# First part's arrays laid out by the host, the second pointwise product's bias as full products, and layer 0's VectorE adaLN tiles as row sums

## The chip, the core and the metric

The kernel runs on one core of a Trainium2 chip. The core has five engines with queues of their own: TensorE (PE, matrix products; its weight loads are listed as PEld), VectorE (DVE), ScalarE (ACT), GpSimd (POOL) and SyncE (SP), which here issues almost all DMAs. They share an on-chip memory (SBUF) of 128 partitions; products go to a second one (PSUM) in banks of 128 x 512 fp32. The metric is the device time of one execution in microseconds; lower is better. The profile is one execution, recorded by the hardware.

## The reference, cut to what matters

A trunk of two layers on 256 tokens of width 2048, all in fp32. Layer 0 mixes tokens by a convolution module, layer 1 by differential attention; both are followed by an MLP of hidden width 8192. Every sub-layer is shifted, scaled and gated by vectors computed from one condition vector c (adaLN):

```python
cond = jax.nn.silu(c)
for i in range(DEPTH):
    mod = cond @ ada_w[i] + ada_b[i]                 # 2048 x 12288 per layer
    sh_m, sc_m, g_m, sh_f, sc_f, g_f = [m[:, None, :] for m in jnp.split(mod, 6, axis=-1)]
    h = x * (1.0 + sc_m) + sh_m
    y = conformer_conv(h, ...) if i % 2 == 0 else diff_attention(h, ...)
    x = layer_norm(alpha * x + g_m * y, ln_mix_g[i], ln_mix_b[i])
    h = x * (1.0 + sc_f) + sh_f
    y = squared_relu_mlp(h, ...)
    x = layer_norm(alpha * x + g_f * y, ln_ffn_g[i], ln_ffn_b[i])

def conformer_conv(h, w1, b1, w_dw, b_dw, g, b, w2, b2):
    u = h @ w1 + b1                                  # first pointwise product, 2048 -> 4096
    a, gt = jnp.split(u, 2, axis=-1)
    u = a * sigmoid(gt)
    u = depthwise_causal_conv(u, w_dw, width=31) + b_dw
    u = silu(layer_norm(u, g, b))
    return u @ w2 + b2                               # second pointwise product, 2048 -> 2048
```

Most of the work is products with weights that are read once: per layer the adaLN matrix (100 MB), the mixer's weights and the MLP's.

## The kernel before

**Products.** fp32 operands are split into a high part in a faster fp32 format and the rest: ACT casts 128 x 1024 of raw weights to the high part (L552 in the first product, L613 behind it), DVE subtracts to get the low part (L553, L615), and PE adds three products per 128 x 512 tile: high x high, high x low, low x high (L564 to L566, L653 to L656). `mm_parts` and `run_jobs` do this for two tiles of 128 tokens.

**The first part** is written out by hand: the order of PE, DVE, ACT and SP is as in the program text (`manual_schedule`). Because h needs shift and scale of the adaLN first, the 2048 input channels are taken in six slices of 128, 128, 256, 512, 512 and 512 (`SLICES`, s = 0 to 5). For each slice the kernel computes the adaLN shift and scale for its channels, makes h from x, and adds the slice's share of the first pointwise product to sums in SBUF (`add_up`, L1106) for eight groups of 2 x 256 output columns. While PE multiplies slice s, the adaLN tiles of slice s + 1 are worked off at set steps (`PAIR_AT`); at the end of a slice come the mod vectors (`end_ada`) and the next slice's h (`put_h`).

**adaLN tiles** come as raw tiles of 1 MiB, through a list of items (`items`, `load_ahead`, `ada_next`) loaded in order on SP's queue into a few rotating homes. Three ways to work them off stand in the kernel:
- by PE (`ada_slice_steps`, `ada_both_steps`): products of the condition (repeated to 32 columns, `condr`) with the tile, then a transpose and a reduction;
- by DVE in layer 0 (`ada_slice_dve_steps`, L253, L255): multiply each chunk of 128 input rows by its condition value and add into an accumulator of nf x 128 columns; at the end PE sums over partitions with products against ones (L238) and DVE adds the bias. This is used for the scale of slices 4 and 5, and later for g_m (channels 0 to 7), sc_f (all 16) and sh_f (0 to 3): 36 channels of 128 columns;
- by DVE in layer 1 and part of g_f (`ada_steps`, L382): the host has laid the matrix out by output column (`ada_rows`), so one instruction multiplies a 128 x 2048 tile by the condition, broadcast to all partitions, and accumulates each row to one value.

**x** is loaded by tokens, in four pieces (`X_AT`), into z; PE transposes each 128 x 128 piece (`put_h1` L1074, `to_featT` L492); DVE and ACT apply scale and shift from PSUM (L501, L504, L1079), ACT and DVE split the result (`put_split`). Then ACT multiplies z by alpha (`alpha_x`, L1064) for the residual. The small vectors and the taps of the convolution come as rows, in 17 small loads (`load_small`), and are turned to columns by PE (`as_cols` L134, `tap_columns` L949).

**Behind the slices** come the convolution on PE (L880), its LayerNorm and swish, and the second pointwise product (`out_proj` with `pw2`), where DVE and PE work off the rest of layer 0's adaLN tiles. Its bias is added by two products with four rows each (L652: four rows of bias as high and low part, picked by a column of the identity), before each of 4 x 2 accumulations. `add_gated` (L823, L824) multiplies by the gate and adds to z.

From there on the order of PE and DVE is still that of the program text; that of ACT, POOL and SP is chosen by a planner that simulates the program when it is built.

## Time and profile before

| | us |
|---|---|
| median of 3 runs | 2330.64 |
| lowest, highest | 2330.64, 8066.31 |
| the profiled execution, whole | 2329.99 |
| its span (first to last instruction) | 2327.4 |
| PE busy in the span | 2267.9 (97%) |
| DVE busy | 1744.0 (75%) |
| ACT busy | 1085.6 (47%) |
| POOL busy | 148.7 (6%) |
| moved by DMA | 607.53 MB, 261 GB/s over the span |
| mean granted clock of PE | 0.995 |

How to read the profile: a group of instructions is named by its line, engine, operation and tiles (output <- inputs), with partitions x elements; behind it stand the count, the busy time, the mean in ns of one, and the idle time before them with what ended it. Matmuls are pipelined, and the duration of one holds its latency: in a row of them each holds PE for less than its duration. A row of the waits says which engine waited at which line for what: sum in us, times, longest. A row of the chain of waits or of the timeline begins with the start and the length in us. A row of a window gives its ends, its length, then busy time (and count) of PE, PEld, DVE, ACT and POOL, then the granted clock (1.00 is full), the DMA share and GB/s.

### The profile page before, as it was taken

The numbers are of one execution on the slowest core, as the hardware profiler recorded it, in microseconds if no ns is written. First come the engines' busy times: TensorE is split into PE (matmuls) and PEld (weight loads), VectorE is DVE, ScalarE is ACT, GpSimd is POOL, SyncE is SP. The second block draws the span as 40 slices with busy tenths as digits, with TensorE's granted clock in tenths as the row PEclk, the third lists the DMA queues.
The fourth block names the chain that finished last, engine by engine and source line by source line (L and its number), as shares of the span: only waits on it lengthen the run. The fifth ranks groups of instructions, "written<-read, shape, count | busy, mean of one in ns | idle before, by whom it ended". The sixth has DMA issues, their size and how long they took to land.

```text
span 2327.4 us, 28629 instructions
## 1 busy us (share of the span) xinstructions
PE 2267.9 (97%) x11183; PEld 1807.8 (78%) x11183; DVE 1744.0 (75%) x2116; ACT 1085.6 (47%) x1497; POOL 148.7 (6%) x110
## 2 busy tenths in 40 slices
PE   7999989999999999999999999999999999999999
PEld 4676647778788888888878888877788888888886
DVE  5687788878887888877878877887975655655556
ACT  3344674365345345445454445545444443443442
POOL 0000001102200000000004110110310000000000
PEclk9999999999999999999999999999999999999999
DMA  9997489969998988888847665784966556565563
GB/s 343 375 347 284 169 305 377 329 241 340 340 326 302 321 288 317 316 298 308 311 159 260 243 210 180 275 310 156 317 234 211 181 185 199 181 199 189 191 218 108
DMA packets 264319, 607.53 MB, mean 261 GB/s; under 512 B 11105, under 2 KB 24567, under 8 KB 249463
## 3 DMA queue, kind: packets, MB, share of 16 engines
q1 hardware_dynamic: 264040, 605.67, 74.4%
q8 instruction: 87, 1.43, 0.2%
q14 instruction: 48, 0.39, 0.0%
q10 hardware_dynamic: 144, 0.06, 0.0%
HBM read 603.53 MB, written 2.15 MB: 260 GB/s over the span
## 4 chain that ended last, share of the span: by engine, by line
PE 74%; issue 16%; DVE 6%; ACT 2%; DMA 2%; POOL 0%; POOLq 0%; DVEq 0%; ACTq 0%; SPq 0%
PE w_ps L656 18%; PE w_ps L655 18%; PE w_ps L653 18%; DVE wl_w L615 2%; PE pw_ps L653 1%; PE qkv_q_ps L656 1%; PE qkv_q_ps L653 1%; PE qkv_q_ps L655 1%; PE qkv_v_ps L656 1%; PE qkv_v_ps L653 1%; PE qkv_v_ps L655 1%; PE ut L1425 1%; PE pw_ps L656 1%; DVE adaw L382 1%; PE pw_ps L655 1%
## 5 line engine op out<-in xcount | busy, mean ns | idle before, releaser
L615 DVE TENSOR_TENSOR wl_w<-w_w,wh_w 128x1024 fp32r<-128x1024 f32 x510 | 634.4, 1262 | 337.1 <-ACT wh_w L613 336.8
L613 ACT CAST wh_w<-w_w 128x1024 fp32r<-128x1024 f32 x512 | 536.1, 1053 | 693.7 <-PE w_ps L656 524.2
L653 PE MATMUL w_ps<-wh_w,hm_hi 128*128 128x512 f32 x1024 | 402.1, 393 | 2.4 <-ACT hm_hi L474 2.4
L656 PE MATMUL w_ps<-wh_w,hm_lo 128*128 128x512 f32 x1024 | 399.6, 390 | 1.6 <-DVE hm_lo L477 1.6
L655 PE MATMUL w_ps<-wl_w,hm_hi 128*128 128x512 f32 x1024 | 399.5, 390 | 1.5 <-DVE wl_w L615 1.5
L655 PE MATMUL w_ps<-wl_w,u_hi 128*128 128x512 f32 x1024 | 399.0, 390 | 1.2 <-DVE wl_w L615 1.1
L653 PE MATMUL w_ps<-wh_w,u_hi 128*128 128x512 f32 x1024 | 399.5, 390 | 0.0
L656 PE MATMUL w_ps<-wh_w,u_lo 128*128 128x512 f32 x1024 | 398.6, 389 | 0.0
L382 DVE SCALAR_TENSOR_TENSOR adaw<-adaw,cond_rows 128x2048 f32<-128x2048 f32 x108 | 249.9, 2314 | 0.5 <-DMA adaw<-in_ada_rows_dram 0.5
L653 PEld LDWEIGHTS w_ps<-wh_w,hm_hi 128*128 128x128 f32 x1024 | 192.6, 188 | 43.9 <-ACT hm_hi L474 3.9
L656 PEld LDWEIGHTS w_ps<-wh_w,hm_lo 128*128 128x128 f32 x1024 | 192.6, 188 | 42.9 <-DVE hm_lo L477 2.9
L655 PEld LDWEIGHTS w_ps<-wl_w,u_hi 128*128 128x128 f32 x1024 | 192.3, 188 | 42.6 <-DVE wl_w L615 3.1
L655 PEld LDWEIGHTS w_ps<-wl_w,hm_hi 128*128 128x128 f32 x1024 | 192.8, 188 | 41.5 <-DVE wl_w L615 2.4
L653 PEld LDWEIGHTS w_ps<-wh_w,u_hi 128*128 128x128 f32 x1024 | 192.3, 188 | 39.8
L656 PEld LDWEIGHTS w_ps<-wh_w,u_lo 128*128 128x128 f32 x1024 | 192.2, 188 | 39.9
L564 PE MATMUL pw_ps<-wh_pw,h_hi 128*128 128x512 f32 x256 | 107.3, 419 | 9.8 <-ACT wh_pw L552 3.5
L565 PE MATMUL pw_ps<-wl_pw,h_hi 128*128 128x512 f32 x256 | 103.0, 403 | 5.1 <-DVE wl_pw L553 5.1
L566 PE MATMUL pw_ps<-wh_pw,h_lo 128*128 128x512 f32 x256 | 102.2, 399 | 0.0
L553 DVE TENSOR_TENSOR wl_pw<-w_pw,wh_pw 128x1024 fp32r<-128x1024 f32 x64 | 77.5, 1220 | 19.8 <-ACT wh_pw L552 19.7
L552 ACT CAST wh_pw<-w_pw 128x1024 fp32r<-128x1024 f32 x64 | 65.7, 1050 | 41.3 <-PE pw_ps L566 27.4
L564 PEld LDWEIGHTS pw_ps<-wh_pw,h_hi 128*128 128x128 f32 x256 | 49.4, 193 | 40.2 <-issue 16.3
L565 PEld LDWEIGHTS pw_ps<-wl_pw,h_hi 128*128 128x128 f32 x256 | 49.5, 193 | 16.2 <-DVE wl_pw L553 7.2
(372 smaller groups left out, 3125.8 us busy)
## 6 DMA issues: line engine op xcount, KB each, us to landing
w_w<-in_mlp_w_dram SPq DMA_DIRECT2D x256, 1024.0 KB, 5.5
adaw<-in_ada_rows_dram SPq DMA_DIRECT2D x108, 1024.0 KB, 6.7
aw<-in_ada_w_dram SPq DMA_DIRECT2D x40, 1024.0 KB, 9.1
w_pw<-in_conv_pw_w_dram SPq DMA_DIRECT2D x64, 512.0 KB, 10.5
conv_ux<-in_ada_w_dram SPq DMA_DIRECT2D x17, 1024.0 KB, 8.3
w_pw<-in_conv_pw_w_dram SPq DMA_DIRECT2D x16, 1024.0 KB, 5.2
w_qkv_q<-in_attn_qkv_w_dram SPq DMA_DIRECT2D x16, 1024.0 KB, 5.9
w_qkv_k<-in_attn_qkv_w_dram SPq DMA_DIRECT2D x16, 1024.0 KB, 5.1
```

The costliest lines, as they stand in the source:

```text
L382: nc.vector.scalar_tensor_tensor(w, w, 1.0, late["cond"], ALU.mult, ALU.mult, accum_out=st["m"][:, ch:ch + 1])
L552: nc.scalar.copy(hq, rq)
L553: nc.vector.tensor_tensor(lq, rq, hq.bitcast(F32), op=ALU.subtract)
L564: nc.tensor.matmul(pss[t], lhsT=xh, rhs=wh, start=(kc == first), stop=False)
L565: nc.tensor.matmul(pss[t], lhsT=xh, rhs=wl, start=False, stop=False)
L566: nc.tensor.matmul(pss[t], lhsT=xl, rhs=wh, start=False, stop=(kc == last))
L613: nc.scalar.copy(hi, rq)
L615: eng.tensor_tensor(lo, rq, hi.bitcast(F32), op=ALU.subtract)
L653: nc.tensor.matmul(pss[tt], lhsT=xh, rhs=wh, start=(kc == 0 and job["bias"] is None), stop=False)
L655: nc.tensor.matmul(pss[tt], lhsT=xh, rhs=wl, start=False, stop=False)
L656: nc.tensor.matmul(pss[tt], lhsT=xl, rhs=wh, start=False, stop=(kc == nk - 1))
L1425: nc.tensor.transpose(out=pt[:, j * P:(j + 1) * P], in_=us[:, j * P:(j + 1) * P], identity=ident)
```

## The change

- **Layout by the host** (`lay_out`): x also by channels (`x_t`), the small vectors as columns in two arrays (`cols_first`, `cols_rest`), the taps as columns, layer 0's PE adaLN tiles and the first product's weight tiles each as one array of 128 x 2048 in the order of use (8 KB in one piece per partition, where pieces had 512 bytes to 4 KB), and 36 more channels in `ada_rows`.
- **h from x by channels** (`chunk_h`): scale and shift read xT in SBUF; no transposes. xT lies in z's buffer; x by tokens is loaded into z once, at step 9 of the last slice, and not scaled: `add_gated` of the second product multiplies by alpha in its add.
- **Row sums** (`dot`, `ada_slice_dot_steps`): layer 0's 36 DVE channels are worked off as layer 1's, one instruction per tile; the bias is added by DVE right behind the last (`add_bias`). The condition as rows (`cond_rows`) is now made at the start, by 16 products with the identity, instead of being written to memory and read back behind the second product.
- **The bias of the second product**: high part in partitions 0 to 3 and low part in 32 to 35 of a zeroed 128 x 512 tile, and one product with 128 rows (`one` has a 1 in row q and in row 32 + q) instead of two with 4.
- A scratch buffer (`R`) moves to the pool that is opened later.

```diff
-X_AT = {(0, 0): (256, 512), (2, 1): (512, 1024), (3, 4): (1024, 2048)}
+X_AT = {(0, 0): (2, 4), (2, 1): (4, 8), (3, 4): (8, 16)}
...
+def lay_out(inputs):
...
+    return {
+        "cols_first": cols(i["c"], i["ada_b"][0]),
+        "cols_rest": cols(i["ada_b"][1], i["conv_pw1_b"], i["conv_dw_b"], i["conv_ln_g"], i["conv_ln_b"],
+                          i["mlp_b1"], i["ln_mix_g"][0], i["ln_mix_b"][0], i["ln_ffn_g"][0], i["ln_ffn_b"][0],
+                          i["ln_mix_g"][1], i["ln_mix_b"][1], i["mlp_b2"], i["attn_subln_g"]),
+        "x_t": i["x"][0].T.reshape(KC, P, S).transpose(1, 0, 2),
+        "taps_t": taps, "ada_tiles": np.stack(ada),
+        "ada_rows": np.stack([at[l][v, ch] for l, v, ch in row_specs()]), "pw1_tiles": np.stack(pw1),
+    }
...
+    vec0 = const.tile([P, KC + 6 * KC], F32, name="vec0")
+    nc.sync.dma_start(vec0, cols_first)
...
+    cond_rows = const.tile([P, D], F32, name="cond_rows")
+    for q in range(4):
+        pt = mm_bank(f"cond_p{q}")
+        for j in range(4):
+            nc.tensor.matmul(pt[:, j * P:(j + 1) * P], lhsT=cond[:, 4 * q + j:4 * q + j + 1].broadcast_to([P, P]),
+                             rhs=ident, start=True, stop=True)
+        if q % 2:
+            nc.scalar.copy(cond_rows[:, q * NG:(q + 1) * NG], pt)
+        else:
+            nc.vector.tensor_copy(cond_rows[:, q * NG:(q + 1) * NG], pt)
+
+    def dot(w, m, ch):
+
+        nc.vector.scalar_tensor_tensor(w, w, 1.0, cond_rows, ALU.mult, ALU.mult, accum_out=m[:, ch:ch + 1])
+
+    def add_bias(m, i, v, c0, n):
+        nc.vector.tensor_tensor(m[:, c0:c0 + n], m[:, c0:c0 + n], adab[i][:, v * KC + c0:v * KC + c0 + n], op=ALU.add)
...
+    xT = z.rearrange("p t (a n) -> p (t a) n", n=S)
...
-            pt = tp_tile(f"apt_{i}_{v}_{f0}")
-            for f in range(nf):
-                nc.tensor.matmul(pt[:, f:f + 1], lhsT=st["acc"][:, f * P:(f + 1) * P], rhs=ones[:, 0:1],
-                                 start=True, stop=True)
...
-                nc.vector.scalar_tensor_tensor(st["acc"], wv[:, kc % per, :], cond[:, kc:kc + 1],
-                                               st["acc"], ALU.mult, ALU.add)
...
+        def load(ch):
+            st[ch] = ada_raw(f"ad_{v}_{ch}")
+            nc.sync.dma_start(st[ch], ada_rows[ADA_ROWS[0, v, ch]])
...
+        def step(ch):
+            dot(st.pop(ch), m, ch)
+            if ch == f0 + nf - 1 and not first:
+                finish()
...
+    def chunk_h(mul, add, c0, n):
+
+        h32 = [work.tile([P, 1, S], F32, tag="B", name=f"h0_h{c0 + j}") for j in range(n)]
+        for j in range(n):
+            cc = c0 + j
+            if j == 0:
+                nc.vector.tensor_scalar(h32[j][:, 0, :], xT[:, cc, :], mul[:, cc:cc + 1], add[:, cc:cc + 1],
+                                        ALU.mult, ALU.add)
+            else:
+                nc.scalar.activation(h32[j][:, 0, :], xT[:, cc, :], AF.Identity,
+                                     scale=mul[:, cc:cc + 1], bias=add[:, cc:cc + 1])
+        for j in range(n):
+            put_split(hT, c0 + j, 1, 0, S, h32[j])
...
-        rv = raw.rearrange("p (a h n) -> p a h n", a=src.shape[1], h=2)
-        for h in range(2):
-            raws["dma"] = nc.sync.dma_start(rv[:, :, h, :], src[:, :, h, :])
+        raws["dma"] = nc.sync.dma_start(raw, pw1_tiles[n])
...
-        nc.vector.tensor_tensor(z[:, t, sl], z[:, t, sl], tmp, op=ALU.add)
+        if times is None:
+            nc.vector.tensor_tensor(z[:, t, sl], z[:, t, sl], tmp, op=ALU.add)
+        else:
+            nc.vector.scalar_tensor_tensor(z[:, t, sl], z[:, t, sl], times, tmp, ALU.mult, ALU.add)
...
-            nc.scalar.activation(z[:, t, sl], z[:, t, sl], AF.Copy, scale=ALPHA)
...
+        hl = work.tile([P, NG], F32R, tag="X", name="pw2b_hl", bufs=3)
+        nc.gpsimd.memset(hl.bitcast(F32), 0.0)
+        for p0 in (0, 32):
+            with tc.issue_after(raws["dma"].ins):
+                nc.sync.dma_start(rows[p0:p0 + 4, :], conv_pw2_b[0].rearrange("(q n) -> q n", n=NG))
+            nc.scalar.copy(hl[p0:p0 + 4, :], rows[p0:p0 + 4, :])
+        nc.vector.tensor_tensor(hl[32:36, :], rows[32:36, :], hl[32:36, :].bitcast(F32), op=ALU.subtract)
+        one = small.tile([P, 4], F32R, tag="one4", name="one4", bufs=1)
+        nc.vector.tensor_tensor(one, ident[:, 0:4], ident[:, 32:36], op=ALU.add)
...
+                nc.sync.dma_start(vec1, cols_rest)
+                nc.sync.dma_start(wct.rearrange("p a k b -> p (a k b)"), taps_t)
+            elif (s, h) == (5, 9):
+                nc.sync.dma_start(z, x[0].rearrange("(t p) d -> p t d", p=P))
...
-             bias=lambda q: lambda: [(bias0["one"][:, q:q + 1].broadcast_to([4, P]), bias0["hl"][:, n, :])
-                                     for n in range(2)])
+             bias=lambda q: lambda: [(bias0["one"][:, q:q + 1].broadcast_to([P, P]), bias0["hl"])])
...
-        late["cond"] = late["pool"].tile([P, D], F32, tag="acc", name="cond_rows")
-        with tc.issue_after(raws["dma"].ins):
-            nc.sync.dma_start(late["cond"], cond_mem.rearrange("k p -> (k p)").partition_broadcast(P))
...
-            aT = work.tile([P, S], F32, tag="R", name=f"{nm}_aT", bufs=3)
+            aT = late["pool"].tile([P, S], F32, tag="R", name=f"{nm}_aT", bufs=3)
```

More of the change, by code (lines that the diff above doesn't have):

```diff
@@ L60 @@
 ON_ACT = (0, 2, 3, 5, 6, 8, 9, 11, 13, 14)
-DVE_WAIT = 3
 ALPHA = (2.0 * DEPTH) ** 0.25
@@ L73, with ada_specs @@
 PI_IN = 3.1415925
-ADA_ROWS = {key: n for n, key in enumerate([(0, G_F, ch) for ch in range(4, KC)] + [
-    (1, v, ch) for v in range(6) for ch in range(KC)])}
+def ada_specs():
+    out = []
+    for s, (f0, nf) in enumerate(SLICES):
+        if s < BOTH_PE and 2 * nf * P <= NG:
+            out += [("both", f0, nf, a) for a in range(2 * nf)]
+        else:
+            out += [(v, f0, nf, a) for v in ((SC_M, SH_M) if s < BOTH_PE else (SH_M,)) for a in range(nf)]
+    for v, f0, nf in ((G_M, 8, 4), (G_M, 12, 4), (SH_F, 4, 4), (SH_F, 8, 4), (SH_F, 12, 4), (G_F, 0, 4)):
+        out += [(v, f0, nf, a) for a in range(nf)]
+    return out
@@ L271, in ada_slice_steps @@
+            add_bias(m, 0, v, f0, nf)
+        def step(ch):
+            dot(st.pop(ch), m, ch)
+            if ch == f0 + nf - 1 and not first:
+                finish()
+        loads = [lambda ch=ch: load(ch) for ch in range(f0, f0 + nf)]
+        steps = [lambda ch=ch: step(ch) for ch in range(f0, f0 + nf)]
+        return (loads, [[f] for f in steps], finish) if first else (loads, steps)
     def ada_slice_steps(i, v, f0, nf, m, first=False, apart=False):
@@ L1058, in ada_pair @@
         later.append(rest)
-    def alpha_x(q):
-        sl = slice(q * NG, (q + 1) * NG)
-        for t in range(NT):
-            nc.scalar.activation(z[:, t, sl], z[:, t, sl], AF.Copy, scale=ALPHA)
     def end_ada(s):
@@ L1068, in end_ada, with put_h @@
             f()
-    def put_h1(s):
-        c0 = SLICES[s][0]
-        pt = tp_tile(f"h0_t1_{c0}")
-        for t in range(NT):
-            nc.tensor.transpose(out=pt[:, t * P:(t + 1) * P], in_=z[:, t, c0 * P:(c0 + 1) * P], identity=ident)
-        def rest():
-            nc.vector.tensor_scalar(mul[:, c0:c0 + 1], m_sc[:, c0:c0 + 1], 1.0, None, ALU.add)
-            h32 = work.tile([P, 1, S], F32, tag="B", name=f"h0_h1_{c0}")
-            nc.vector.tensor_scalar(h32[:, 0, :], pt[:, :S], mul[:, c0:c0 + 1], m_sh[:, c0:c0 + 1],
-                                    ALU.mult, ALU.add)
-            put_split(hT, c0, 1, 0, S, h32)
-        return rest
-    def put_h(s, c2, now=True):
-        f0, nf = SLICES[s]
-        made = put_h1(s) if nf == 1 else to_featT(z, hT, mul, m_sh, "h0", [c2])
-        def rest():
-            if nf > 1 and 2 * c2 == f0:
-                nc.vector.tensor_scalar(mul[:, f0:f0 + nf], m_sc[:, f0:f0 + nf], 1.0, None, ALU.add)
-            made()
-            if nf > 1 and c2 % 2:
-                later.append(lambda: alpha_x(c2 // 2))
-        if now:
-            rest()
-        return rest
+    def put_h(s, c2):
+        f0, nf = SLICES[s]
+        c0, n = (f0, 1) if nf == 1 else (2 * c2, 2)
+        if c0 == f0:
+            nc.vector.tensor_scalar(mul[:, f0:f0 + nf], m_sc[:, f0:f0 + nf], 1.0, None, ALU.add)
+        chunk_h(mul, m_sh, c0, n)
     def add_up(g, s, pss):
@@ L1129, in pw2_bias @@
     def pw2_bias():
[L1131 to L1138 removed]
+        rows = work.tile([P, NG], F32, tag="bc_b2", name="pw2b", bufs=1)
+        hl = work.tile([P, NG], F32R, tag="X", name="pw2b_hl", bufs=3)
[7 more added lines that the diff above has]
+        nc.vector.tensor_tensor(one, ident[:, 0:4], ident[:, 32:36], op=ALU.add)
         bias0.update(hl=hl, one=one)
@@ L1206, in trunk @@
                 split_half(s)
-            if s == 3 and 5 <= h < 9:
-                tap_columns(h - 5)
-            elif (s, h) == (3, 9):
-                conv_vectors()
+            if (s, h) == (3, 5):
+                nc.vector.tensor_reduce(eye, ident.rearrange("p (r c) -> p c r", c=32), axis=AX.X, op=ALU.add)
             if h in PAIR_AT[s]:
@@ L1319, in ln_t, with out_proj @@
         return [stats, norm]
-    def out_proj(pair, w2d, gate, name, pump, at_end, start=None, hold=False, on_pool=((),) * 4, bias=None):
+    def out_proj(pair, w2d, gate, name, pump, at_end, start=None, hold=False, on_pool=((),) * 4, bias=None,
+                 times=None):
         st = stats_tile(name)
@@ L1722, in fin_begin @@
         fin["zg"] = big.tile([P, NT, D], F32, tag="hTl", name="fin_zg")
-        fin["rows"] = late["pool"].tile([P, D], F32, tag="acc", name="fin_rows")[0:2]
+        fin["rows"] = cond_rows[0:2]
         fin["cols"] = small.tile([P, NT, 2], F32, tag="fcol", name="fin_cols", bufs=1)
```

236 lines of the change are left out of this document (62 added, 174 removed).

## The prediction

> **What bounds the kernel now.** I read the page first (spans, the chain), then the busy time by stage, then the waits of TensorE inside the first stages, and last single stretches of the timeline.
>
> ```profile
> span 2327.4 us, 28629 instructions
> PE 2267.9 (97%) x11183; PEld 1807.8 (78%) x11183; DVE 1744.0 (75%) x2116; ACT 1085.6 (47%) x1497; POOL 148.7 (6%) x110
> PE 74%; issue 16%; DVE 6%; ACT 2%; DMA 2%; POOL 0%; POOLq 0%; DVEq 0%; ACTq 0%; SPq 0%
> ```
>
> TensorE (PE) carries three quarters of the chain of waits. The "issue" share is the opening: there the chain has one unbroken piece (2.62 us to 344 us) and tells nothing, so that part has to be read by windows. The cuts below are the start (to 23 us), the slices of the first product (to 290), the convolution's end (to 346), the second pointwise product with its adaLN tiles (to 455), and the rest.
>
> ```profile
> 0.00:23.00 23.00, 11.39 (x51) 6.67 (x52) 8.04 (x17) 7.55 (x11) 2.02 (x12) 1.00 1.01 294
> 23.00:175.00 152.00, 144.22 (x722) 101.36 (x721) 118.23 (x175) 60.47 (x86) 0.00 (x0) 0.98 1.02 364
> 175.00:290.00 115.00, 109.74 (x878) 77.30 (x880) 90.72 (x155) 63.57 (x100) 0.00 (x0) 1.00 0.61 224
> 290.00:346.00 56.00, 50.77 (x684) 27.03 (x677) 47.47 (x94) 40.25 (x72) 0.71 (x1) 0.97 0.81 301
> 346.00:455.00 109.00, 106.29 (x510) 79.13 (x509) 95.12 (x98) 44.88 (x58) 15.31 (x5) 0.98 1.00 371
> 455.00:2327.40 1872.40, 1845.53 (x8350) 1516.28 (x8348) 1384.41 (x1579) 868.83 (x1174) 130.61 (x92) 1.00 0.71 247
> ```
>
> After the bounds: length, then busy time of PE, weight load, VectorE (DVE), ScalarE (ACT), GpSimd (POOL), granted clock, DMA share, GB/s. Everything the change touches lies before 455 us or just behind it. There PE is busy nearly throughout from 23 us on; DMA is full too until 175 us (share 1.02); VectorE has 78% to 87%. Which of the three sets the pace shows in what PE waits for. These are the waits of PE, and the one of ACT on weights, between 23 and 346 us (sum, times, longest):
>
> ```profile
> PE pw_ps L565 <- DVE wl_pw L553: 4.6, 4, 1.7
> PE pw_ps L564 <- DVE sums L1106: 3.5, 4, 2.3
> PE cv L880 <- ACT vtok L895: 2.6, 1, 2.6
> PE pw_ps L564 <- ACT h_hi L474: 1.1, 1, 1.1
> PE pw_ps L564 <- ACT wh_pw L552: 1.1, 2, 0.7
> PE pw_ps L564 <- DVE conv_ux L920: 0.9, 1, 0.9
> ACT wh_pw L552 <- DMA w_pw<-in_conv_pw_w_dram: 3.7, 3, 1.7
> ```
>
> PE itself never waits for a transfer there, and the split of the weights waits 3.7 us for one in 323 us: the DMA is full because it runs ahead, not because somebody starves. PE is the bound, interrupted by VectorE's queue (the three DVE rows, 9.0 us) and by ScalarE at the ends of slices and of the convolution (4.8 us). So an instruction taken off PE counts nearly in full, one taken off VectorE counts by its share in those waits, and a faster transfer counts only at the start.
>
> **The change, part by part.**
>
> *Products with ones (L238).* The old VectorE tiles summed over chunks of rows and left the sum over partitions to PE, which the row sums make needless.
>
> ```profile
> L238 PE MATMUL apt<-ones,aacc x72: 164/250/271, 133.6 to 452.5; 128*128 128x1 f32 x72
> 366.95 1.68 PE apt L238 x16
> ```
>
> The second row is from the chain: sixteen in 1.68 us, 0.105 us each. 72 x 0.105 = 7.6 us of PE goes.
>
> *Transposes.* x arrives transposed, and vectors and taps as columns.
>
> ```profile
> L492 PE MATMUL h_t<-ident,z x28: 270/272/273, 47.9 to 193.8; 128*128 128x128 f32 x28
> L1074 PE MATMUL h_t<-ident,z 128*128 128x128 f32 x4 | 1.0, 348 | 0.0
> L949 PE MATMUL wct_p<-ident,taps 124*128 124x124 f32 x4 | 0.6, 269 | 0.0
> L134 PE MATMUL pt_conv<-ident,small_rows 80*128 80x80 f32 x1 | 0.2, 233 | 0.0
> 499.40 0.87 PE ut L1425 x8
> ```
>
> The last row is the price when they run in line: 0.87/8 = 0.109 us. Gone are 28 + 4 of x, 4 of the taps and five like pt_conv (the two at the start lie in waiting time): 41 x 0.109 = 4.5 us.
>
> *The bias.* Two products with four rows become one with 128 rows, for each of 4 column groups and 2 token tiles.
>
> ```profile
> L652 PE MATMUL pw_ps<-pw2b_hl,one x16: 383/440/497, 350.3 to 437.2; 4*128 4x512 f32 x16
> 384.28 0.66 PE pw_ps L652 x2
> 365.13 0.23 PE pw_ps L653
> ```
>
> A pair holds PE 0.66 us; an ordinary 128-row product holds it 0.23 us. I price the new one like that: 8 x (0.66 - 0.23) = 3.4 us. No row shows a product whose stationary side is one column repeated; the bound from the nearest row is half a pair, 0.33 us, and then 2.6 us is saved. The Trainium skill (TensorE: Matmul & The Clock Gate, section Why this matters for your kernels) says that a single matmul with 32 rows takes the same time as one with 128. By that rule only the count would matter, 8 x 0.23 = 1.8 us, and the sum would be 1.6 us smaller; this trace disagrees, with 0.33 us for four rows against 0.23 us for 128.
>
> *VectorE.* 36 channels of layer 0 change form: 12 in slices of 512 columns (four instructions a channel), 24 in slices of 1024 (two a channel).
>
> ```profile
> L255 DVE SCALAR_TENSOR_TENSOR aacc<-aw,cond,aacc 128x512 f32<-128x512 f32 x18 | 13.5, 750 | 0.4
> L255 DVE SCALAR_TENSOR_TENSOR aacc<-aw,cond,aacc 128x1024 f32<-128x1024 f32 x26 | 35.3, 1357 | 0.5
> L382 DVE SCALAR_TENSOR_TENSOR adaw<-adaw,cond_rows 128x2048 f32<-128x2048 f32 x108 | 249.9, 2314 | 0.5 <-DMA adaw<-in_ada_rows_dram 0.5
> L382 DVE DVE_READ_ACCUMULATOR adaw<-adaw,cond_rows x108: 71/82/88, 495.7 to 1685.0; 128x1 f32 x108
> ```
>
> A channel cost 4 x 0.750 = 3.00 or 2 x 1.357 = 2.71 us; as a row sum, as layer 1 has them already, 2.31 + 0.08 = 2.40 us. Saved: 12 x 0.60 + 24 x 0.31 = 14.6 us of VectorE. It counts where PE waits for VectorE, 9.0 us in the rows above. I take a third of that, 3.0 us (an estimate: the waits come at slice ends behind an adaLN step, which gets shorter by a tenth to a fifth, and the chain of h loses its transposes and its reads from PSUM); bounds 0 and 9.0.
>
> *Clock.* Such waits also cost afterwards.
>
> ```profile
> 52.00:56.00 4.00, 2.05 (x5) 1.71 (x6) 3.55 (x7) 4.00 (x8) 0.00 (x0) 0.74 1.05 386
> 56.00:60.00 4.00, 4.00 (x16) 3.23 (x16) 3.99 (x5) 1.65 (x2) 0.00 (x0) 0.83 1.05 385
> 360.00:364.00 4.00, 3.10 (x11) 1.32 (x12) 4.00 (x4) 0.89 (x2) 2.47 (x1) 0.64 1.03 412
> ```
>
> Behind the 2.3 us wait the clock fell: 4 x 0.26 + 4 x 0.17 = 1.7 us lost. By the granted clock of the stages (0.98 of 152 us, 0.97 of 56, 0.98 of 109) there are some four such falls before 455 us. I expect one fewer: 1.7 us; bounds none (0) and all (6.8).
>
> *The start.* Better transfers against more PE work.
>
> ```profile
> 1.17 3.91 SPq L326 DMA_DIRECT2D aw_bNone<-in_ada_w_dram  x4
> 3.48 0.43 DVE L170 COPY condr<-cond 128x512 f32<-128x512 f32 x1
> 10.80 1.94 PE L333 MATMUL aps_b<-aw_bNone,condr 128*32 128x256 f32 x16 [1.64 <-DMA aw_bNone<-in_ada_w_dram]
> 16.73 0.79 PE L564 MATMUL pw_ps<-wh_pw,h_hi 128*128 128x512 f32 x1 [2.39 <-ACT wh_pw L552]
> ```
>
> The first slice's 2 MiB, issued from 1.17 us, have landed at 10.80 us in pieces of 512 bytes, while the whole stretch moved 294 GB/s. At the 386 GB/s of 52 to 56 us the difference is 2.1 MB/294 - 2.1 MB/386 = 1.7 us earlier. Against it, cond_rows puts 16 fp32 products (two records each, as L238's 36 products have 72) on PE between 3.5 us and the first tile. At the in-line 0.109 us they take 3.5 us and are over when the first tile comes; at double that, cold, 7.0 us, until 10.5 us; then both tiles' products (2 x 1.94 us) follow and end at 14.4 instead of 12.7 us: 1.7 us lost. I take 0, between +1.7 and -1.7.
>
> *At nothing.* x is loaded a second time, 2 MiB by tokens, in the last slice: 5.4 us of DMA at 386 GB/s, in a stage where the DMA share is 0.61; its buffer was last read by the slice before, so SP's queue behind it (weights and adaLN tiles) isn't held, and z as tokens is first used by the second product's gated add. Without that cover it would delay the weights by 5.4 us. SP issues 2 loads instead of 17 small ones. ACT loses the scaling of z and the tap copies, and only 1.1 us of PE's waits name its casts. The later read-back of cond (1 MiB) goes; the row sums of layer 1 wait for nothing in its place. The gated add becomes a three-operand form, 0.75 instead of 0.69 us by L255's row, eight times: 0.5 us of VectorE beside PE. POOL gets one memset, in a stage where it does next to nothing.
>
> **Sum.** 7.6 + 4.5 + 3.4 + 3.0 + 1.7 = 20.2 us. The profiled execution took 2329.99 us (span 2327.4), 0.65 us under the median of 2330.64; I predict 2329.99 - 20.2, some 2310 us.
>
> **Rivals.**
>
> *The transfers are the bound until 175 us and again in the second product.* For it: DMA shares of 1.02 and 1.00, and 412 GB/s reached at 360 us in pieces of 2 and 4 KB, so longer rows could go faster still. Then 152 us shrink by 364/412 to 134 and 109 us by 371/412 to 98: 18 + 11 = 29 us, with 1.7 at the start and PE's share of 175 to 346 us (some 4 us): 2295 us. Against: the 3.7 us. The Trainium skill (DMA: Bandwidth & Descriptors, section Specifications) gives some 358 GB/s as HBM's limit for a core; by that nothing could be gained here, but the 386 and 412 of this trace are above it. 18 in 100.
>
> *The removed PE work only widens waits.* At each slice end PE waits for the chain of h, so a transpose or product gone there just lets it wait longer; VectorE at 87% in 346 to 455 us takes over there. Then the bias and half of the 12.1 us of products and transposes remain: 9 us, 2321 us. For it: VectorE's 95.1 of 109 us; against: no DVE wait on PE's list is over 2.3 us. 20 in 100.
>
> *PE loses its clock more often, and the kernel is slower.* Less PE work between unchanged chains makes gaps longer, each over some 2 us costs 1.7 us more. The place is the convolution's end, 16 steps of products, with VectorE at 85%. It decides from twelve more falls on, 12 x 1.7 = 20.4 us against the 20.2 saved; with all 16 it is 2330 + 7 = 2337 us. Against: only four falls now, and what feeds those chains gets shorter too. 10 in 100, a little of it for a worse order of ACT and POOL behind 455 us.
>
> *The change doesn't do what it says*: row sums blocking VectorE 2.3 us at a time where two halves stood (2 x 0.75 before the shift's products, 2 x 0.75 behind): 8 steps in slices 4 and 5, each delaying a split by up to 0.8 us, 6.4 us lost of the sum: 2316 us. It is inside the forecast's range.
>
> **The numbers.** Forecast (2302 to 2318, the last rival in it) 52 in 100; transfers 18; wait-widening 20; slower 10. The range leaves out the far end of the first and most of the last: low 2292 is 2310 less the other bounds of VectorE (6.0), clock (5.1), the start (1.7) and ScalarE's 4.8; high 2328 leaves the bias alone with the start's loss (2330 - 3.4 + 1.7). A change of 2% (47 us), about what a measurement of this kernel can tell from no change, needs more than any case gives: faster by over 2% 0.03, for transfers and PE's gains adding up; slower by over 2% 0.02; within 0.95.
>
> **What would show it.** L238, L492, L1074, L949 and L134 are gone, and PE's records fall by 72 + 43 + 8 less 32 added. Between 23 and 346 us the stretch is shorter by the products, transposes and waits there, some 11 us; from the first bias product to the first product of the MLP some 8 us less. Row sums of layer 0 are near 2.3 us. Wrong would be: a stretch to 175 us that shrinks with the GB/s at an unchanged list of waits (transfers were the bound), longer waits of PE on DVE with the same stage lengths (the second rival), or granted clocks under 0.95 in 290 to 346 us (the third). From 455 us on lengths should agree within 2 us.

## The result and the profile after

| us | before | after |
|---|---|---|
| median of 4 runs | 2331.05 | 2304.28 |
| lowest | 2330.64 | 2302.94 |
| the profiled execution, whole | 2329.99 | 2303.69 |
| its span | 2327.4 | 2301.9 |

The ratio is 0.9889, with a 95% interval of 0.987 to 0.9909: 26.8 us shorter, where 20.2 were predicted, and within 2%. (One execution of the kernel before took 8066 us; it was disturbed, and the ratio leaves it out.)

The page of the changed kernel: busy time of the engines, and the chain of waits by engine.

```profile
PE 2251.6 (98%) x11092; PEld 1798.7 (78%) x11092; DVE 1729.9 (75%) x2083; ACT 1079.1 (47%) x1478; POOL 153.5 (7%) x110
...
PE 82%; DVE 9%; issue 4%; ACT 3%; DMA 1%; POOL 0%; POOLq 0%; SPq 0%; ACTq 0%; DVEq 0%
```

PE has lost 91 records, 11183 to 11092, just the 72 + 43 + 8 - 32 of the prediction, and is still the bound.

Where the time went is read best between the same points of the work. I take the first and the last high x high tile of the first product, the first of the second product, and the first of the MLP. These are the rows of those groups, with duration (lowest/median/highest, ns) and start of the first and the last in us; first the kernel before:

```profile
L564 PE MATMUL pw_ps<-wh_pw,h_hi x256: 387/393/792, 16.7 to 270.1; 128*128 128x512 f32 x128
L653 PE MATMUL pw_ps<-wh_pw,swish_hi x128: 389/389/796, 351.0 to 460.7; 128*128 128x512 f32 x128
L653 PE MATMUL w_ps<-wh_w,hm_hi x1024: 387/389/628, 467.6 to 2225.6; 128*128 128x512 f32 x171
```

And the changed kernel:

```profile
L562 PE MATMUL pw_ps<-wh_pw,h_hi x256: 387/390/793, 14.3 to 257.0; 128*128 128x512 f32 x128
L651 PE MATMUL pw_ps<-wh_pw,swish_hi x128: 388/389/501, 334.2 to 436.1; 128*128 128x512 f32 x128
L651 PE MATMUL w_ps<-wh_w,hm_hi x1024: 387/389/632, 444.7 to 2199.7; 128*128 128x512 f32 x171
```

The start is 2.4 us shorter, the MLP begins 22.9 us earlier (467.6 to 444.7), and the span is 25.5 us shorter. Cut at these points (each stage's end 0.4 us behind the start of its last tile), the windows are as follows, in the prediction's columns: bounds, length, busy time of PE, PEld, DVE, ACT, POOL, granted clock, DMA share, GB/s. Slices, convolution, second product; before:

```profile
16.70:270.50 253.80, 240.26 (x1308) 171.77 (x1309) 197.71 (x299) 110.46 (x158) 0.00 (x0) 0.99 0.87 311
270.50:351.00 80.50, 74.55 (x1015) 40.22 (x1013) 68.08 (x137) 62.51 (x111) 0.71 (x1) 0.98 0.76 284
351.00:467.60 116.60, 112.22 (x539) 84.31 (x538) 100.45 (x113) 46.66 (x59) 16.16 (x7) 0.99 0.96 352
```

After, and below them the stretch to 175 us as the prediction cut it:

```profile
14.30:257.40 243.10, 232.27 (x1253) 164.92 (x1254) 188.40 (x274) 102.03 (x138) 0.00 (x0) 0.98 0.83 335
257.40:334.20 76.80, 71.04 (x996) 37.51 (x995) 67.37 (x139) 62.83 (x111) 1.23 (x2) 0.98 0.77 300
334.20:444.70 110.50, 104.12 (x492) 79.00 (x490) 96.72 (x110) 46.72 (x60) 19.09 (x7) 0.98 0.96 370
...
23.00:175.00 152.00, 145.46 (x720) 101.25 (x719) 114.62 (x159) 55.46 (x71) 0.00 (x0) 0.99 0.96 391
```

The slices lost 10.7 us, the convolution 3.7, the second product 6.1. VectorE's busy time over the three fell from 366.2 to 352.5 us: 13.7, where 14.6 were predicted. PE's fell by 19.6 us, and the time in which it was idle stayed what it was (450.9 - 427.0 = 23.9 us before, 430.4 - 407.4 = 23.0 after). So the removed work came off the path and was not replaced by waits. That is a sum over three stages; the experiments show that part by part it is less tidy.

The waits of PE from 20 to 330 us, and the one of ACT for the weights, after:

```profile
PE pw_ps L563 <- DVE wl_pw L551: 3.2, 3, 1.3
PE pw_ps L562 <- DVE sums L1044: 2.9, 3, 1.8
PE cv L880 <- ACT conv_ux L862: 2.8, 1, 2.8
...
ACT wh_pw L550 <- DMA w_pw<-in_pw_tiles_dram: 7.0, 1, 7.0
```

The two long VectorE rows went from 8.1 (4.6 + 3.5) to 6.1 us; the rest is as it was. ACT now waits longer for weights, once, and the casts behind it cost PE 0.4 us in all (a row not shown).

**How much the same work varies.** Behind the first MLP tile no kernel of this study was edited, except for where some buffers lie. From there to the end the fourteen profiled executions took 1857.2 us (the changed kernel: 2301.9 - 444.7) to 1868.3 us. So 11 us of scatter lie there, and the changed kernel's record is its lower end. In the slices two kernels that differ from the changed one only in the bias took 241.4 and 242.7 us against 243.1. Ahead of the MLP much of the scatter is the clock: from 23 us to the MLP the records have one to four falls of the granted clock, each to half for 3.4 us (1.7 us lost) or twice that, together 1.3 to 6.8 us lost. Below I therefore read stages, not medians, and take nothing under some 2 us for shown; a difference at the MLP of up to 5 us can be the clock alone. By the ratios alone only `dve_old` (slower) and `dots_short` (faster) lie clear of the changed kernel's interval.

### The profile page after: what moved, and what is told of

The parts are those of the page before. It is cut to its first block, busy times and chain, and to the rows that moved or that the text cites. A ratio compares the mean times of both kernels' runs of the same rounds, so it can differ in the third digit from the quotient of the medians.

```text
span 2301.9 us, 28283 instructions
## 1 busy us (share of the span) xinstructions
PE 2251.6 (98%) x11092; PEld 1798.7 (78%) x11092; DVE 1729.9 (75%) x2083; ACT 1079.1 (47%) x1478; POOL 153.5 (7%) x110
## 4 chain that ended last, share of the span: by engine, by line
PE 82%; DVE 9%; issue 4%; ACT 3%; DMA 1%; POOL 0%; POOLq 0%; SPq 0%; ACTq 0%; DVEq 0%
PE w_ps L651 19%; PE w_ps L654 19%; PE w_ps L653 19%; PE pw_ps L562 2%; PE pw_ps L563 2%; PE pw_ps L564 2%; PE qkv_v_ps L654 1%; PE qkv_v_ps L651 1%; PE qkv_v_ps L653 1%; PE qkv_q_ps L654 1%; PE qkv_q_ps L651 1%; PE qkv_q_ps L653 1%; PE ut L1354 1%; DVE adaw L210 1%; DVE wl_w L613 1%
## 5 line engine op out<-in xcount | busy, mean ns | idle before, releaser
L562 PEld LDWEIGHTS pw_ps<-wh_pw,h_hi 128*128 128x128 f32 x256 | 49.1, 192 | 39.2 <-issue 14.4
L563 PEld LDWEIGHTS pw_ps<-wl_pw,h_hi 128*128 128x128 f32 x256 | 49.2, 192 | 14.8 <-DVE wl_pw L551 5.6
```

The lines of the kernel that those rows point to most:

```text
L562: nc.tensor.matmul(pss[t], lhsT=xh, rhs=wh, start=(kc == first), stop=False)
L563: nc.tensor.matmul(pss[t], lhsT=xh, rhs=wl, start=False, stop=False)
```

## The experiments

Each kernel is the changed kernel with one part put back or one cost altered. "At the MLP" is the start of its first MLP tile against 444.7 us.

**The layout by the host put back** (`old_layout`): the adaLN tiles of PE and the first product's weights come in pieces of 512 bytes to 4 KB again.

```diff
-            nc.sync.dma_start(t, ada_tiles[ADA_AT[v, f0, nf, a]])
+            tv = t.rearrange("p (j n) -> p j n", n=w)
+            nc.sync.dma_start(tv, av[:, per * a:per * (a + 1), n0:n0 + w])
...
-        raws["dma"] = nc.sync.dma_start(raw, pw1_tiles[n])
+        for h in range(2):
+            raws["dma"] = nc.sync.dma_start(rv[:, :, h, :], src[:, :, h, :])
```

> The changed kernel, with the host's order undone for layer 0's PE adaLN tiles and the first product's weights alone (pieces of 512 bytes to 4 KB again). If PE is the bound, only the start gets longer: the second adaLN tile lands near 10.8 us again and the first pointwise product starts near 16.7 instead of 14.3 us; the last product of the slices moves from 257 to about 259.5 us and the kernel takes about 2306 us (2304 to 2308). If transfers were the bound until 175 us, most of that stretch's gain goes: the last product of the slices stands near 267 to 270 us and the kernel takes 2314 us or more.

Measured: 2311.25 us, ratio to before 0.9911 [0.9896, 0.9926]. Its slices (from its first tile on), the stretch to 175 us, and its wait for weights:

```profile
15.50:260.80 245.30, 232.35 (x1253) 164.84 (x1254) 188.51 (x274) 102.10 (x138) 0.00 (x0) 0.98 0.91 333
...
23.00:175.00 152.00, 143.84 (x712) 99.75 (x711) 113.78 (x158) 53.48 (x69) 0.00 (x0) 0.99 1.04 391
...
ACT wh_pw L559 <- DMA w_pw<-in_conv_pw_w_dram: 14.4, 5, 7.5
```

It starts 1.2 us later (15.5 against 14.3), is 2.2 us longer in the slices, and is 3.9 us later at the MLP, of which 1.7 are the clock, which stands at half for longer on the way. At the start some 0.6 us are the layout's: the second tile's adaLN products end 2.4 instead of 1.9 us behind the condition's products. The rest is those products themselves, which no layout touches; they took 6.35 us here and 5.83 in the changed kernel, and from 5.2 to 6.7 in the other records that have them at the start. Old pieces and new rows move the same 391 GB/s up to 175 us, with the DMA busy 1.04 and 0.96 of the time: longer rows need less of the DMA's time, but PE asks for no more. With transfers as the bound, 18 us would have had to come back by 175 us and 29 in all. That rival is out.

**Layer 0's VectorE tiles in the old form** (`dve_old`), with the products of ones, and with the condition as rows written to memory at the start and read back behind the second product for layer 1; then (`dve_old2`) the same with two accumulators in place of one:

```diff
-            loads, steps = ada_slice_dot_steps(v, f0, nf, m, False)
+            loads, steps = ada_slice_dve_steps(0, v, f0, nf, m, False)
...
-            sc = ada_slice_dot_steps(SC_M, f0, nf, m_sc)
+            sc = ada_slice_dve_steps(0, SC_M, f0, nf, m_sc)
```

```diff
-                st["acc"] = pool.tile([P, 2 * NG], F32, tag=tag, name=f"aacc_{i}_{v}_{f0}", bufs=1)[:, :w]
+                st["acc"] = pool.tile([P, 2 * NG], F32, tag=tag, name=f"aacc_{i}_{v}_{f0}", bufs=2 if f0 == 0 else 1)[:, :w]
```

> The changed kernel with layer 0's 36 VectorE channels in the old form (accumulate over chunks of rows, then products with ones on PE); cond as rows is written to memory and read back behind the second product. If PE's own work is the price: 72 records of 0.105 us, 7.6 us, and some 3 us for VectorE, so about 2315 us (2312 to 2317), of which 4 to 5 us lie between the first bias product and the MLP. If only VectorE's waits count (products with ones fall into waits): about 2307 us. If VectorE is the bound in the second product: 2319 us or more.

> The old form of layer 0's VectorE channels again, but with two accumulators in turn for the slices that begin at channel 0 (g_m, then sc_f), so that VectorE needn't wait 5.0 us near the convolution's end until PE's products with ones have read the first. If that coupling, with the clock falls behind it, is what the old form costs above PE's own 2 us, 3 to 5 us of its 11 go: about 2312 us. If the cost is VectorE's 15 us of additional work, or the clock for another reason, nothing goes: 2316 us.

Measured: 2316.3 us (0.9931 [0.9916, 0.9946]) with one accumulator, 2310.91 us (0.9912 [0.9898, 0.9927]) with two. Windows of the convolution and of the second product, a wait of VectorE, and one of PE behind it, with one:

```profile
257.60:341.70 84.10, 77.37 (x1012) 42.20 (x1012) 69.47 (x139) 63.95 (x113) 1.23 (x2) 0.94 0.74 285
341.70:454.90 113.20, 107.85 (x532) 83.23 (x530) 100.17 (x114) 45.68 (x57) 15.18 (x7) 0.99 0.93 353
...
DVE aacc L329 <- PE apt L314: 5.0, 1, 5.0
PE cv L935 <- DVE conv_ux L919: 3.3, 2, 3.0
```

With two accumulators VectorE has no such wait:

```profile
257.40:332.50 75.10, 71.22 (x1012) 39.07 (x1012) 67.90 (x138) 62.60 (x111) 1.23 (x2) 1.00 0.78 304
332.50:447.10 114.60, 108.45 (x533) 84.31 (x531) 100.74 (x113) 46.97 (x59) 14.01 (x7) 0.99 0.95 359
```

And the kernel before:

```profile
DVE aacc L253 <- PE apt L238: 5.0, 1, 5.0
```

The old form is 10.2 us later at the MLP with one accumulator and 2.4 with two. The difference, 7.8 us, lies in the convolution (84.1 against 75.1 us). It hangs on one wait that the kernel before had as well: VectorE, about to begin the next tile's sum, waits 5.0 us until PE has read the accumulator of the last one; that read was put three steps later in PE's order. Behind VectorE in its order stand the convolution's inputs. With the granted clock taken out (84.1 x 0.94 = 79.1, 75.1 x 1.00, and 76.8 x 0.98 = 75.3 for the changed kernel) some 4 us are the wait itself, and 5.0 are the clock (84.1 - 79.1), which fell three times in the stage with one accumulator and not at all with two. The kernel before agrees with the 4 us: it has the same hand-over, one fall in this stage as the changed kernel has, and a convolution that is 3.7 us longer. So that a row sum has no accumulator to hand over is worth some 4 us, not 7.8, and the change gained at most the 3.7 us of this stage by it. Even that isn't seen directly on PE: its idle time in the stage was 6.0 us before and is 5.8 now, with one long wait each (2.6 and 2.8 us). In the slices the old form takes as long (242.3 us with one accumulator, 243.0 with two, against 243.1), but at a clock of 0.99 against 0.98, which is some 2 us; so it may cost that much there.

**The products with ones alone** (`ones_dummy`): 72 records on PE at the old places, on columns of the condition, which nobody reads; the row sums stay.

```diff
+        def products():
+            pt = tp_tile(f"apt_0_{v}_{f0}")
+            for f in range(nf):
+                nc.tensor.matmul(pt[:, f:f + 1], lhsT=cond_rows[:, f * P:(f + 1) * P], rhs=ones[:, 0:1],
+                                 start=True, stop=True)
```

> The changed kernel plus the 36 old products with ones (72 records) at their old places, on a tile that stands ready, with nobody waiting for their result: PE's price of them alone. If each record holds PE 0.105 us on the path, 7.6 us: 2312 us, of it 1.7 us in the slices, 1.7 in the convolution and 4.2 between the first bias product and the MLP. If most fall into waits, as the slices of the run with the old form say (nothing lost until 257 us), 2 to 4 us: 2306 to 2308 us, and the rest of that run's 11 us came from VectorE waiting for PE and PE for VectorE around them.

Measured: 2307.58 us (0.9891 [0.9875, 0.9908]). Slices, convolution, second product:

```profile
15.00:258.60 243.60, 233.56 (x1269) 166.99 (x1270) 188.39 (x274) 102.03 (x138) 0.00 (x0) 0.98 0.83 333
258.60:333.00 74.40, 70.94 (x1012) 38.40 (x1011) 67.40 (x138) 62.72 (x111) 1.24 (x2) 1.00 0.78 307
333.00:446.10 113.10, 108.20 (x532) 84.00 (x530) 94.44 (x104) 46.82 (x59) 16.71 (x7) 0.98 0.94 363
```

0.5 us in the slices, 2.6 in the second product; the convolution was even shorter, with a clock of 1.00 for 0.98. At the MLP it is 1.4 us later. Of the predicted 7.6 us some 3 at most are there; the other products fall into time in which PE waits anyway.

**VectorE nearly without layer 0's row sums** (`dots_short`): each is taken over 64 columns of 2048. This leaves out most of the sum, so the shift, scale and gate values are not the reference's; only its time counts.

```diff
+        if short:
+            nc.vector.scalar_tensor_tensor(w[:, :64], w[:, :64], 1.0, cond_rows[:, :64], ALU.mult, ALU.mult,
+                                           accum_out=m[:, ch:ch + 1])
+            return
...
-            dot(st.pop(ch), m, ch)
+            dot(st.pop(ch), m, ch, True)
```

> The changed kernel with layer 0's 36 row sums cut to 64 of 2048 columns (so these modulation values are not the reference's): some 80 us less of VectorE, the loads unchanged. If PE is the bound and VectorE counts only in waits, at most the listed waits go: 3 to 7 us, 2297 to 2301 us. If VectorE is the bound of the convolution's end or of the second product, 15 us or more go: under 2290 us.

Measured: 2296.24 us (0.9842 [0.9828, 0.9857]). The same three stages:

```profile
15.00:252.10 237.10, 228.68 (x1253) 163.00 (x1254) 162.20 (x277) 101.95 (x138) 0.00 (x0) 0.99 0.86 342
252.10:325.70 73.60, 69.28 (x998) 36.78 (x997) 48.08 (x134) 62.56 (x111) 1.24 (x2) 1.00 0.83 324
325.70:431.30 105.60, 103.21 (x492) 78.83 (x490) 63.61 (x110) 46.82 (x59) 14.25 (x7) 0.99 0.97 379
```

VectorE has 78.6 us less to do (26.2 + 19.3 + 33.1), and the stages are 14.1 us shorter (6.0 + 3.2 + 4.9): 0.18 us for each. In this record the clock also fell two times less than in the changed kernel's, which is 3.4 us; without them it is 10.7 us, 0.14 for each. VectorE is not the bound, but what comes off it counts by about a sixth or a seventh. 14.6 us at these rates are 2.0 to 2.6; the prediction took 3.0.

**x by tokens again** (`x_old`: transposes on PE and scaling by alpha on ACT as before; `x_tok`: without the scaling, which stays in the gated add):

```diff
-    def chunk_h(mul, add, c0, n):
+    def to_featT(src, pair, mul, add, name, c2s):
...
+                    nc.tensor.transpose(out=pts[c2][:, j * S + t * P: j * S + (t + 1) * P],
+                                        in_=src[:, t, cc * P:(cc + 1) * P], identity=ident)
```

> The changed kernel with x loaded by tokens, transposed by PE, and scaled by alpha on ACT as before; everything else new. If PE's own work is the price: 32 transposes of 0.109 us, 3.5 us, so about 2308 us (2306 to 2310), spread over the slices. If the chain that makes h at the five slice ends is the price (PSUM reads, the scaling of z ahead of the casts), each end is longer by 1 to 2 us and the kernel takes 2310 to 2315 us.

> x by tokens and PE's transposes as in the run with the old x, but alpha stays in the gated add, so ACT doesn't scale z in the slices. If the scaling ahead of the casts is what made the slices 6.9 us longer there (3.5 us were expected of the transposes), they are now 3 to 4 us longer than in the changed kernel, the last product of the slices near 260.5 us. If it is the transposes and the reads from PSUM, they stay near 264 us.

Measured: 2310.22 us (0.9909 [0.9893, 0.9926]) and 2312.08 us (0.9916 [0.9898, 0.9935]). The slices, first with the scaling, then without:

```profile
15.00:264.30 249.30, 237.83 (x1283) 169.38 (x1284) 190.02 (x274) 105.73 (x146) 0.00 (x0) 0.97 0.80 317
```

```profile
15.10:264.80 249.70, 237.75 (x1283) 169.37 (x1284) 189.94 (x274) 101.57 (x138) 0.00 (x0) 0.97 0.80 316
```

6.2 and 6.6 us longer than 243.1, whether ACT scales or not (it is 4 us busier in the first): the scaling costs nothing, the transposes do, with the reads from PSUM behind them. Priced at 3.5 us, they cost some 4.5 and one more fall of the clock at 144 us, about 1.7. At the MLP they are 4.1 and 7.4 us later; with the scaling the convolution happened to keep its full clock.

**The vectors and taps as rows again** (`vec_old`): the small loads and the transposes of `as_cols` and `tap_columns`.

```diff
-                nc.sync.dma_start(vec1, cols_rest)
-                nc.sync.dma_start(wct.rearrange("p a k b -> p (a k b)"), taps_t)
+                load_small(0, "conv", [conv_pw1_b[0], conv_dw_b[0], conv_ln_g[0], conv_ln_b[0]])
+                nc.sync.dma_start(taps, conv_dw_w[0].rearrange("k (q c) -> (k q) c", q=4))
```

> The changed kernel with the small vectors (but for c and layer 0's adaLN bias) and the taps as rows again: 17 small loads, PE's transposes, and the copies of VectorE and ACT. By PE's own price, 9 transposes of 0.109 us: 1.0 us, 2305 us. What the other three undone parts and the bias leave of the gain until the MLP is near 3 us; if this part holds it, the slices end near 260 us and the kernel takes 2307 us.

Measured: 2305.06 us (0.9882 [0.9865, 0.9899]), 1.3 us later at the MLP: near the predicted 1.0, and below what the runs can tell from nothing.

**The bias** in two other forms: two products with four rows, as before (`bias_two`), and one with 36 rows (`bias_36`).

```diff
-             bias=lambda q: lambda: [(bias0["one"][:, q:q + 1].broadcast_to([P, P]), bias0["hl"])])
+             bias=lambda q: lambda: [(bias0["one"][:, q:q + 1].broadcast_to([4, P]), bias0["hl"][:, n, :])
+                                     for n in range(2)])
```

```diff
-             bias=lambda q: lambda: [(bias0["one"][:, q:q + 1].broadcast_to([P, P]), bias0["hl"])])
+             bias=lambda q: lambda: [(bias0["one"][0:36, q:q + 1].broadcast_to([36, P]), bias0["hl"][0:36])])
```

> The changed kernel with the bias as two products of four rows again. By the rows before, a pair holds PE 0.66 us against 0.23 us: 3.4 us, 2307.5 us, all of it between the first bias product and the MLP. If the number of rows doesn't matter, the eight products more cost 0.23 us each: 1.8 us, 2306 us.

> The changed kernel with the one bias product on the 36 rows that hold anything, not on 128. If few rows are what made the old product hold PE for 0.33 us, it does so here too, and the eight cost 0.8 us more than now. If the number of rows doesn't matter, each holds PE 0.23 us as now, and the old price came from two such products in a row.

Measured: 2309.59 us (0.9901 [0.9882, 0.992]), and 2310.41 us in the one execution of the second. From the timeline of PE (start, length, instruction): the changed kernel, with 128 rows,

```profile
334.69 0.40 PE L654 MATMUL pw_ps<-wh_pw,swish_lo 128*128 128x512 f32 x1
334.92 0.40 PE L650 MATMUL pw_ps<-pw2b_hl,one 128*128 128x512 f32 x1
335.15 0.39 PE L651 MATMUL pw_ps<-wh_pw,swish_hi 128*128 128x512 f32 x1
335.39 0.39 PE L653 MATMUL pw_ps<-wl_pw,swish_hi 128*128 128x512 f32 x1
```

with 36,

```profile
333.81 0.40 PE L654 MATMUL pw_ps<-wh_pw,swish_lo 128*128 128x512 f32 x1
334.13 0.49 PE L650 MATMUL pw_ps<-pw2b_hl,one 36*128 36x512 f32 x1
334.56 0.50 PE L651 MATMUL pw_ps<-wh_pw,swish_hi 128*128 128x512 f32 x1
334.89 0.39 PE L653 MATMUL pw_ps<-wl_pw,swish_hi 128*128 128x512 f32 x1
```

and with two times four:

```profile
333.21 0.40 PE L654 MATMUL pw_ps<-wh_pw,swish_lo 128*128 128x512 f32 x1
333.54 0.73 PE L650 MATMUL pw_ps<-pw2b_hl,one 4*128 4x512 f32 x2
334.20 0.50 PE L651 MATMUL pw_ps<-wh_pw,swish_hi 128*128 128x512 f32 x1
334.54 0.39 PE L653 MATMUL pw_ps<-wl_pw,swish_hi 128*128 128x512 f32 x1
```

From the start of the product ahead to the start of the second one behind: 0.70, 1.08 and 1.33 us. With 128 rows the steps are 0.23 us throughout. A product with fewer rows takes longer itself (0.43 with 36, 0.33 each with four), and so do its two neighbours, by 0.1 us each. So a pair given up is worth 0.63 us of PE's time, and 0.43 where the bias product stands behind adaLN products of another shape, since the step behind it is longer there with 128 rows too: 5 x 0.63 + 3 x 0.43 = 4.4 us, more than the predicted 3.4.

What costs it is not settled. Above 0.23 us for each product, one of 36 rows costs 0.4 us (1.08 - 0.70) and two of four rows cost 0.4 us together (1.33 - 0.93). So it can be the row count, or the change of shape between neighbours. The changed kernel's first bias product, one of those behind adaLN products, steps 0.34 us:

```profile
333.89 0.49 PE L650 MATMUL pw_ps<-pw2b_hl,one 128*128 128x512 f32 x1
334.23 0.39 PE L651 MATMUL pw_ps<-wh_pw,swish_hi 128*128 128x512 f32 x1
```

No run has a longer row of products with few rows, which would tell the two apart. Less than half of the 4.4 us reached the stage: the stretch from the second product's first tile to its last became 1.8 us shorter (103.7 us with two products, 103.3 with 36 rows, 101.9 changed), since PE waits more in the same stage: of its window (one tile longer than the stretch) PE is idle 1.6 us with two products and 4.0 changed. The windows, two products first:

```profile
332.60:436.70 104.10, 102.46 (x466) 76.79 (x466) 89.32 (x92) 41.60 (x52) 19.10 (x6) 1.00 0.99 382
```

```profile
334.20:436.50 102.30, 98.30 (x459) 76.36 (x458) 89.41 (x92) 41.94 (x52) 18.16 (x6) 1.00 1.01 389
```

By the MLP not even that is left: in the changed kernel's record the clock fell at 440 us, in these two it did not.

**The condition's products taken out of the start** (`cond_spread`), into the first slices; and **two more of the convolution's steps given from VectorE to ACT** (`shift_act`), as an attempt at a faster kernel:

```diff
+            if h == 0 and 1 <= s <= 3:
+                cond_quarter(s)
```

```diff
-ON_ACT = (0, 2, 3, 5, 6, 8, 9, 11, 13, 14)
+ON_ACT = (0, 1, 2, 3, 5, 6, 8, 9, 10, 11, 13, 14)
```

> The changed kernel with the 16 products that spread cond to rows taken from the start and put, four at a time, where PE waits for h: ahead of the first product of slices 0 to 3. If they hold up the start (they end at 8.9 us and the first adaLN products follow at 8.8 us), the first product starts earlier by 1 to 2 us, the rest lies in waits of 1.1 to 2.6 us, and the kernel takes about 2302 us (2300 to 2303). If the landing of the tiles sets the start, nothing moves there (2304 us), and if they widen the waits instead of filling them, up to 3.5 us are lost: 2308 us.

> The changed kernel with 12 instead of 10 of the convolution's 16 shifted copies per group on ACT, 4 on VectorE: 16 copies of 0.45 us less on VectorE (7.2 us), 10.7 us more on ACT, in the stretch from 190 to 303 us. By what 80 us less of VectorE gave (8.6 us until the convolution's end, some 0.1 us each), 1 us or less is gained: 2303 us. If VectorE's place in the chains of the convolution is what PE waits for, 3 us or more: 2301 us, faster than both. If ACT's copies (0.67 us each) stand in those chains, it is slower: 2306 us.

Measured: 2305.73 us (0.9892 [0.9869, 0.9915]) and 2307.32 us (0.9901 [0.9881, 0.9922]). Neither gains. With `shift_act` the slices are 2.6 us shorter (240.5) and the convolution 2.3 us longer (79.1, at a clock of 0.96 against 0.98). Without the condition's products the first tile of the first product came no earlier, at 14.8 us against 14.3. The rows say why. The start of the changed kernel:

```profile
3.06 5.83 PE L201 MATMUL cond_p<-ident,cond 128*128 128x128 f32 x32 [3.06 <-DVE cond L192]
...
8.82 1.93 PE L348 MATMUL aps_b<-aw_bNone,condr 128*32 128x256 f32 x32
```

And that of `cond_spread`:

```profile
9.02 1.93 PE L349 MATMUL aps_b<-aw_bNone,condr 128*32 128x256 f32 x16 [0.48 <-DMA aw_bNone<-in_ada_tiles_dram]
```

Behind the condition's products 32 adaLN products take 1.93 us, without them 16 do. What the new work delays, it also speeds up.

## Why the prediction was right, and where its terms were not

The total was right to within the range (2304.3 in 2292 to 2328, 5.7 us under the forecast), and the bound was read rightly. Its sum was not right term by term:

| term | predicted | runs, at the MLP or in the stage |
|---|---|---|
| products with ones | 7.6 | 1.4 to 3.1 |
| accumulator handed over to PE | not priced | some 4, and 7.8 with the clock falls of `dve_old` |
| x's transposes | 3.5 | 4.1 to 7.4 |
| vectors and taps | 1.0 | 1.3 |
| bias | 3.4 | 1.8 in the stage, 0 at the MLP |
| VectorE's shorter form | 3.0 | 2.0 to 2.6 |
| clock, one fall fewer | 1.7 | see below |
| the start | 0 | 2.4 |
| layout behind the start | 0 | 2.7, of it 1.7 the clock |

Put back one by one, layout, row sums, x and vectors come to 3.9 + 10.2 + 4.1 (or 7.4) + 1.3 = 19.5 (or 22.8) of the 22.9 us at the MLP. Each of these figures holds its record's draw of clock falls, so that the sum comes out so near says little. Shown beyond the scatter are the transposes (twice, in the slices), the hand-over, and the rate of VectorE's work; the layout and the vectors are not.

- **Products with ones** is the term that failed: "72 x 0.105 = 7.6 us of PE goes" took a price from a place where they ran in line. In the slices and the convolution they mostly lie in waits. The rival of widened waits is right for this part, though not for the sum, since PE's idle time did not grow.
- **The hand-over.** The step list said nothing of VectorE waiting for PE, because only PE's waits were listed. VectorE's list for the kernel before has the 5.0 us row above. It is an edge of the very instructions that the change removes, and the two forms of the old code show that it was worth some 4 us. Products priced some 5 us too dear, and a hand-over, transposes, a start and a layout priced too cheap or at nothing, cancelled. That the total came out well is in this part luck.
- **Transposes** were rightly counted at 0.109 us each, and mis-sized: beside PE's time there is the chain of h at slice ends, which the prediction put into VectorE's term.
- **The bias.** That 128 rows cost an ordinary 0.23 us was right, and giving up a pair was worth 0.43 to 0.63 us of PE's time. The Trainium skill (TensorE: Matmul & The Clock Gate, section Why this matters for your kernels) has 32 rows take the time of 128; the 36-row steps of 0.43 us against 0.23 speak against it here, for single products between others of 128 rows. What failed is the step from PE's time to the stage's: the second product isn't bound by PE alone.
- **VectorE**: "a third of that, 3.0 us" is near the measured rate.
- **The start**: the price of the two tiles' products, 2 x 1.94 us, was that of the kernel before, where they came first on PE. Now they took 1.93 together. Some 0.6 us of the 2.4 are the layout's; the rest, these products and the h without transposes, was not tried apart, and the start of kernels that don't differ in it varies by 1.4 us (13.8 to 15.2).
- **At nothing**: the second load of x, the lost scaling and the small loads moved nothing that shows. The layout behind the start was taken for hidden; 2.7 us were measured, of which 1.7 are the clock, so no gain is shown.
- **Stages**: 11 us were forecast between 23 and 346 us, and slices and convolution lost 14.4. From the first bias product (350.3 and 333.9 us) to the MLP 8 were forecast, and 6.5 went (117.3 to 110.8). Behind the MLP's first tile 2.6 us went, where 2 was the limit behind 455 us; that part varies by 11 us by itself.
- **Rivals.** Transfers: out, by `old_layout`. More clock loss: out; from the first tile on no stage is under 0.98 (the mark was 0.95). Row sums that block VectorE: no trace of it, as `dve_old` has no shorter slices beyond the scatter (242.3 against 243.1).

**The clock.** Between the first tile and the MLP there were four falls before (52, 93, 319 and 360 us) and three after (50, 303 and 440), so one fewer, as forecast. (Left out of the count are the first tiles, which both kernels run at half the clock: the products stand 0.43 us apart until 22.8 us before and 20.8 us after. The 1.00 in the windows of the kernel before says nothing there, since its clock records begin at 23.2 us.) But the gain of one fall was not earned by an edit, as this pair shows: PE waiting at the same instruction for the same 1.80 us, with the window behind it. The changed kernel:

```profile
50.57 0.47 PE L562 MATMUL pw_ps<-wh_pw,h_hi 128*128 128x512 f32 x1 [1.80 <-DVE sums L1044]
...
50.00:54.00 4.00, 3.43 (x10) 2.75 (x11) 4.00 (x6) 2.18 (x3) 0.00 (x0) 0.71 1.01 416
```

And `dots_short`:

```profile
51.67 0.47 PE L566 MATMUL pw_ps<-wh_pw,h_hi 128*128 128x512 f32 x1 [1.80 <-DVE sums L1048]
...
52.00:56.00 4.00, 4.00 (x19) 3.33 (x18) 4.00 (x6) 2.33 (x3) 0.00 (x0) 1.00 1.02 420
```

The one wait cost its clock and the other didn't. Nor is this pair alone: shortly ahead of the MLP's first tile PE waits for ACT (at the products `hm_t`) in each of the fourteen records, always for 2.38 or 2.39 us; behind that wait the clock fell in nine of them and stayed full in five. A term "one fall fewer" is a draw of 1.7 us, not a gain that can be worked out. What decides it stays open.

## What to carry to other kernels

When an edit changes the form of a step, list the waits of every engine that touches its buffers, not only those of the bound: a single accumulator that another engine has to read was worth some 4 us, the instructions that read it at most 3. A price taken in line holds only where the bound engine has no waits around it; in stages with waits, small pieces of work fall into them. A study of a per cent is read by stages that the edit touches, with the scatter of untouched stages as the measure, and with the falls of the clock counted in both records before their lengths are compared.
